# One unbroken run for a pair's step, three silu buffers, a tenth raw buffer, and gathers that begin later

## The chip, the cores and the metric

The kernel runs on one core of a Trainium2 chip, as one launch. The metric is device time in microseconds (us). Three runs of the kernel before gave 1726.6, 1728.15 and 1728.6 us, median 1728.15 us. A fourth execution was profiled: 1726.18 us, of which the profile spans 1724.4 us, at a mean granted TensorE clock of 0.989. In texts and rows PE is TensorE, DVE is VectorE, ACT is ScalarE, POOL is GpSimd and SP is SyncE; L171 is line 171 of the kernel before.

## The reference

A trunk of two layers over 256 tokens of width 1024. Only the end of the second layer is changed, a mixture of experts, top 2 of 8, each expert a SwiGLU of width 3584:

```
def _moe(h, router_w, wg, wu, wd):
    t = h.reshape(b * s, d)
    logits = einsum('td,de->te', t, router_w)
    vals, idx = lax.top_k(logits, TOP_K)
    w = jax.nn.softmax(vals, axis=-1)
    gate = sum(one_hot(idx, N_EXPERTS) * w[..., None], axis=1)
    for e in range(N_EXPERTS):
        y = y + gate[:, e:e+1] * (silu(t @ wg[e]) * (t @ wu[e])) @ wd[e]
...
        x = x + _moe(h, router_w[j], exp_w_gate[j], exp_w_up[j], exp_w_down[j])
    return _rms_norm(x, norm_final_g)
```

Before it stand a mixer with four branches in each layer and a dense SwiGLU in the first layer; they end at about 842 us of the span and are the same in both kernels.

## The kernel before

**Tiling.** The device counts the tokens of each expert and sorts the experts by load (`in_places`). The four largest, `q[0]` to `q[3]`, are taken singly, with up to 128 token places each. The four smallest are taken as two pairs, `p[0]` and `p[1]`, 64 places an expert. An expert's work is seven steps `c` (512 of the 3584 columns). A step needs its gate weights, its up weights and its down weights, each in two pieces of 1 MB (128 x 2048 f32): six pieces for a single expert, twelve for a pair. With 28 single steps and 14 pair steps that makes 336 pieces. `PAIRS` says where pair steps stand: after the single steps number 2, 4, ... 26 and 27. The last step is `p[1]`, c=6.

**Weights.** `Stream` loads pieces in the order of `pieces(steps)` from SP's queue into a ring of raw buffers: four of `rawp` and `NX`=5 of `rawx`, nine in all. A single expert's piece is split: ACT copies it to `wh` (L164), DVE subtracts to `wl` (L171), with three buffers of each, and then its raw buffer is free; PE makes three products of each 128 rows (`mm3`, L196, L197, L198). A pair's piece is used raw (`rawn`, loaded at L1088) by PE in fp32 (L1302), and its buffer is free after the last of its products. Two pieces are begun ahead of the products in work (`ahead=2`). The last 14 pieces are loaded in quarters, so 56 loads of 256 KB.

**Order.** PE, ACT and DVE run in the order in which the program is written (`manual_schedule`), so an instruction that waits holds up all that is written behind it on its engine. A step of the loop (L1361) is: gate products, silu (L1372), transposes of the previous step's result (`act_T`, L243 and the copies L214 or L1319), up products, multiplication, then the down products of the previous step, whichever kind that was. Between the pieces `tick()` runs one of the waiting `units`: eight parts of a gather (L1222), the comparison that makes the selection matrix `dm` (L1207), its transposes and gate values (`back`, L1244, L1253), or a scatter of a finished expert's output (L1335).

**The ends.** The first expert's tokens are gathered in one go (`gather_now`: 32 products, 8 copies by ACT) once both halves of the tokens are routed. In step 0 stand `in_places()`, `gates()` and the first `back`. Three groups are gathered later: `p[0]` with `q[1]` from step (q0,0), `p[1]` with `q[2]` from (q1,3), and `q[3]` from (q2,3). At the end come the last down products (`p[1]`, c=6), a Sqrt on ACT (L1393, ahead of them), the last scatters, the final norm and four output transfers on SP (L1418).

Of the kernel before, what the change touches and what calls it, by code (L numbers as in the profile page):

```python
# [34 lines left out]
NX = 5  # L35
# [29 lines left out]
def trunk(ctx: ExitStack, tc: tile.TileContext, x, pos, invf, rows, cols, wst, w_a, w_kvf, w_gate, w_br,  # L65
# [863 lines left out]
    class Routed:  # L929
# [48 lines left out]
        def meanwhile(self, pmm, psp, step):  # L978
# [4 lines left out]
            elif step == 1:  # L983
                self.products(1, 0, 4)
                self.finish(0, 1)
                self.tokens(0)
                self.gained(0, 1)
            elif step == 2:
                self.products(0, 4, 8)
                self.choose(0)  # L990
            else:
                self.wps = [psp.tile([P, 512], F32, tag="sm", name="wps") for _ in range(NT)]
                for t in range(NT):
                    nc.tensor.matmul(self.wps[t][:, :NE], ones if t else excl, self.sel[:, 0], start=True, stop=not t)
                self.place(0)
                self.tokens_hi(0)
                self.tokens_lo(0)

        def end(self, psp):
# [6 lines left out]
            nc.tensor.matmul(self.wps[1][:, :NE], excl, self.sel[:, 1], start=False, stop=True)  # L1006
            self.begin(self.third, hi=True)
            self.place(1)
# [19 lines left out]
        def place(self, t):  # L1028

            nc.vector.scalar_tensor_tensor(self.where[:, t], self.wps[t][:, :NE], 1.0, self.sel[:, t], op0=OP.add,  # L1030
                                           op1=OP.mult)

            if t == 0:
                self.dm = const.tile([P, NT, 2, P], F32R, tag="dm", name="dm")
# [15 lines left out]
    def experts(l, mine):  # L1050
# [3 lines left out]
        with ExitStack() as c2:  # L1054
# [3 lines left out]
            gf = lw.tile([P, D], F32, name="gf")  # L1058
            nc.sync.dma_start(gf, bass.AP(tensor=gfin.tensor, offset=gfin.offset, ap=[[0, P], [1, D]]))
# [5 lines left out]
            class Stream:  # L1065
# [3 lines left out]
                def __init__(self, srcs, ahead=2, whole=False):  # L1069
                    self.srcs, self.begun, self.ready, self.ahead = list(srcs), [], [], ahead  # L1070
                    self.whole = whole

                def begin(self):
                    (w, q, *rest), parts = self.srcs.pop(0)
# [7 lines left out]
                    if q < NB or self.whole:  # L1082
                        self.begun.append(load_hi(src, parts=parts, pool=pool))
                    else:
                        raw = pool.tile([P, 4 * W], F32, tag="raw", name="rawn")
                        n = 4 * W // parts
                        for i in range(parts):
                            nc.sync.dma_start(raw[:, i * n:i * n + n], src[:, i * n:i * n + n])  # L1088
                        self.begun.append(raw.rearrange("p (k n) -> p k n", k=4))

                def fill(self):
                    while (self.srcs or self.begun) and len(self.ready) <= self.ahead:
                        if not self.begun:
                            self.begin()
                        b = self.begun.pop(0)
                        self.ready.append(load_lo(*b) if isinstance(b, tuple) else b)

                def get(self):
                    self.fill()
                    return self.ready.pop(0)  # L1100
# [58 lines left out]
            class Expert:  # L1159
# [3 lines left out]
                def __init__(self, *at, base=0):  # L1163
                    self.at, self.pair, self.base = at, len(at) > 1, base
                    self.y = [None, None]
# [12 lines left out]
            def run(steps, groups, stream, tagx):  # L1178


                with ExitStack() as c3:
# [13 lines left out]
                    def slots_of(group):  # L1195


                        dm = const.tile([P, NT, 2, P], F32R, tag="dm", name="dm")
                        for i, x in enumerate(group):
                            n = P // len(x.at)  # L1200
                            for j, q in enumerate(x.at):
                                wc = whereq[:, :, q:q + 1]
                                if x.base:
                                    ws = const.tile([P, NT, 1], F32, tag="ws", name="ws")
# [313 lines left out]
```

## Time and profile before

| | |
|---|---|
| median of three runs | 1728.15 us |
| profiled execution, its own time | 1726.18 us |
| its span | 1724.4 us |
| PE busy | 1675.1 us (97%) |
| DVE busy | 1054.3 us (61%) |
| ACT busy | 830.5 us (48%) |
| bytes moved by DMA | 497.69 MB, mean 289 GB/s |

The busy shares are means over stages of different kinds. The profile page cuts the span into 40 equal slices of 43.1 us and gives for each the busy share of every engine and the GB/s that the DMA engines moved; the experts take the slices from the 20th on. The chain of waits is read backwards from the last instruction: at each step it names what the instruction waited for. A timeline lists an engine's instructions with their start, their time and, in brackets, the idle time before them and what ended it. An fp32 product of PE is recorded twice, so 16 products stand as x32.

### The profile page before, as it was taken

To read this page: it belongs to the slowest core of one execution; us is meant where nothing else is said; L and a number is where in the kernel's file an instruction comes from. 1 tells how busy PE (TensorE), PEld (TensorE's weight loads), DVE (VectorE), ACT (ScalarE), POOL (GpSimd) and SP (SyncE) were. 2 spreads that over 40 slices of the span, in tenths; PEclk is the share of its full clock that TensorE was granted. 3 is DMA by queue.
4 is the path that set the end of the run, shared out by engine and by line. 5 is a ranking of instruction groups with operands and counts; after the bars stand their busy time and mean duration, and the time that the engine had idled before them with its cause. 6 is when DMAs were issued, how large, how long until landed. Compare 5 with 4: busy or idle time off the path is not lost.

```text
span 1724.4 us, 20366 instructions
## 1 busy us (share of the span) xinstructions
PE 1675.1 (97%) x7800; PEld 1215.4 (70%) x7800; DVE 1054.3 (61%) x1282; ACT 830.5 (48%) x884; POOL 12.1 (1%) x28
## 2 busy tenths in 40 slices
PE   8999999999999999999999999999999999999996
PEld 6888888888887888888776565656656565655652
DVE  6779976555545678986675455536456544735534
ACT  6656454544434566445474444435444443534433
POOL 1000000000000000000000000000000000000000
PEclk9999999999999999999899999999999999999998
DMA  7444445555553643454668999999999999999996
GB/s 274 171 147 146 172 149 193 196 185 181 176 190 123 244 147 123 171 183 175 277 244 322 421 421 422 421 421 418 416 421 421 421 421 421 421 421 421 421 397 231
DMA packets 77818, 497.69 MB, mean 289 GB/s; under 512 B 8752, under 2 KB 8800, under 8 KB 20368
## 3 DMA queue, kind: packets, MB, share of 16 engines
q1 hardware_dynamic: 76752, 493.45, 72.8%
q0 software_dynamic: 960, 2.85, 0.6%
q8 instruction: 63, 1.03, 0.2%
q14 instruction: 43, 0.35, 0.1%
HBM read 495.22 MB, written 1.05 MB: 288 GB/s over the span
## 4 chain that ended last, share of the span: by engine, by line
PE 47%; DMA 9%; DVE 4%; ACT 3%; issue 1%; ACTq 0%; SPq 0%; DVEq 0%
DMA raw<-in_e_d 5%; PE yps L1302 4%; PE gps L1302 4%; PE ups L1302 3%; PE zps L196 3%; PE zps L198 3%; PE zps L197 3%; PE gps L196 3%; PE gps L197 3%; PE yps L197 3%; DVE wl L171 3%; PE gps L198 2%; PE yps L196 2%; PE yps L198 2%; ACT wh L164 2%; PE ups L196 2%
## 5 line engine op out<-in xcount | busy, mean ns | idle before, releaser
L171 DVE TENSOR_TENSOR wl<-raw,wh 128x2048 fp32r<-128x2048 f32 (+1 forms) x312 | 681.9, 2195 | 342.4 <-ACT wh L164 342.2
L164 ACT ACTIVATE wh<-raw 128x2048 fp32r<-128x2048 f32 (+1 forms) x312 | 571.1, 1838 | 406.1 <-PE zps L198 76.4
L196 PE MATMUL zps<-wh,hh 128*128 128x512 f32 (+1 forms) x544 | 215.7, 397 | 2.9 <-ACT wh L214 1.7
L197 PE MATMUL zps<-wl,hh 128*128 128x512 f32 (+1 forms) x544 | 209.5, 385 | 0.9 <-DVE wl L215 0.9
L198 PE MATMUL zps<-wh,hl 128*128 128x512 f32 (+1 forms) x544 | 209.6, 385 | 0.0
L215 DVE TENSOR_TENSOR al<-ps_t,ah 128x512 fp32r<-128x512 f32 x42 | 28.4, 688 | 181.0 <-ACT ah L214 180.8
L196 PEld LDWEIGHTS zps<-wh,hh 128*128 128x128 f32 x544 | 102.7, 189 | 23.7 <-ACT wh L214 2.1
L1372 ACT ACTIVATE act<-gps 128x512 f32<-128x512 f32 x42 | 25.1, 598 | 195.0 <-PE gps L1302 171.7
L197 PEld LDWEIGHTS zps<-wl,hh 128*128 128x128 f32 x544 | 102.7, 189 | 21.4 <-DVE wl L215 2.5
L198 PEld LDWEIGHTS zps<-wh,hl 128*128 128x128 f32 x544 | 102.5, 188 | 20.7
L1302 PE MATMUL ups<-rawn,xs 128*64 128x512 f32 x448 | 101.6, 597 | 1.6 <-DMA rawn<-in_e_u 1.6
L503 DVE SCALAR_TENSOR_TENSOR cacc<-ypad,col,cacc 128x256 f32<-128x256 f32 x240 | 101.4, 478 | 0.0
L1302 PE MATMUL yps<-rawn,aT 128*64 128x512 f32 x448 | 100.3, 596 | 0.0
L1302 PE MATMUL gps<-rawn,xs 128*64 128x512 f32 x448 | 100.3, 596 | 0.0
L197 PE MATMUL yps<-wl,ah 128*128 128x512 f32 x224 | 91.4, 408 | 6.7 <-DVE wl L171 6.5
L196 PE MATMUL yps<-wh,ah 128*128 128x512 f32 x224 | 92.0, 411 | 2.0 <-ACT wh L164 2.0
L196 PE MATMUL ups<-wh,xb 128*128 128x512 f32 x224 | 91.6, 409 | 0.0
L197 PE MATMUL gps<-wl,xb 128*128 128x512 f32 x224 | 88.8, 397 | 2.2 <-DVE wl L171 2.0
L198 PE MATMUL yps<-wh,al 128*128 128x512 f32 x224 | 90.4, 404 | 0.0
L196 PE MATMUL gps<-wh,xb 128*128 128x512 f32 x224 | 90.1, 402 | 0.0
L198 PE MATMUL ups<-wh,xb 128*128 128x512 f32 x224 | 88.6, 395 | 0.0
L198 PE MATMUL gps<-wh,xb 128*128 128x512 f32 x224 | 88.4, 394 | 0.0
(311 smaller groups left out, 2408.6 us busy)
## 6 DMA issues: line engine op xcount, KB each, us to landing
raw<-in_e_g SPq DMA_DIRECT2D x56, 1024.0 KB, 13.6
raw<-in_e_u SPq DMA_DIRECT2D x56, 1024.0 KB, 13.6
raw<-in_e_d SPq DMA_DIRECT2D x54, 1024.0 KB, 11.9
rawn<-in_e_g SPq DMA_DIRECT2D x52, 1024.0 KB, 12.7
rawn<-in_e_u SPq DMA_DIRECT2D x52, 1024.0 KB, 16.2
rawn<-in_e_d SPq DMA_DIRECT2D x52, 1024.0 KB, 14.1
raw<-in_w_gate SPq DMA_DIRECT2D x32, 1024.0 KB, 4.7
raw<-in_w_a SPq DMA_DIRECT2D x28, 1024.0 KB, 4.8
```

Source lines behind the costliest of these rows:

```text
L164: nc.scalar.activation(hi[:, sl], raw[:, sl], AF.Copy)
L171: nc.vector.tensor_sub(lo[:, sl], raw[:, sl], hi[:, sl].bitcast(F32))
L196: nc.tensor.matmul(ps, xh, wh, start=first, stop=False)
L197: nc.tensor.matmul(ps, xh, wl, start=False, stop=False)
L198: nc.tensor.matmul(ps, xl, wh, start=False, stop=last)
L215: nc.vector.tensor_sub(lo, src, hi.bitcast(F32))
L503: nc.vector.scalar_tensor_tensor(cacc[:, b], src, wcol, cacc[:, b], op0=OP.mult, op1=OP.add)
L1302: nc.tensor.matmul(ps[js], lhs(k)[:, js], w[:, kk], start=k == 0, stop=k == ktot - 1)
L1372: nc.scalar.activation(a, gps, AF.Silu)
```

## The change

A pair's step becomes one run: its own previous down products, then its gate, then its up products, twelve pieces with nothing between them. The single steps keep their form (gate, transposes, up, down of the previous single step); the transposes of the pair's result are made in the single step behind it. Silu's results get three buffers, the ring a tenth raw buffer (`NX`=6). The first gather's units are queued at the end of step 0 and not in it; `gates()` moves to step 1 and the first `back` behind that gather; `p[1]` is gathered alone from (q2,1) and `q[2]` alone from (q1,3). `gather_now` makes the products of the first token half ahead of the second half's places, in four PSUM banks, and ACT and DVE share the copies. A loop sees to it that an expert's gather is complete before its first product. Quarters are used for the last 6 pieces. At the end the Sqrt stands ahead of the last single step's transposes and down products. The gain vector of the final norm is loaded at the end, and two of the four output transfers go out by ACT's queue. Names at new lines: L1318 are the raw fp32 products, L1211 the comparison (tile `dms`), L1335 the copy of a pair's transposes, L1381 silu, L1435 the Sqrt.

```
-NX = 5
+NX = 6
...
             def pieces(steps):
-                order, last = [], None
-                down = lambda x, c: [(e_d, q, c, dc) for dc in range(2) for q in x.at]
+                order, last = [], [[], []]
                 for x, c in steps:
-                    order += [(w, q, c, h) for w in (e_g, e_u) for h in range(2) for q in x.at]
-                    if last:
-                        order += down(*last)
-                    last = x, c
-                return order + down(*last)
+                    into = [(w, q, c, h) for w in (e_g, e_u) for h in range(2) for q in x.at]
+                    order += last[1] + into if x.pair else into + last[0]
+                    last[x.pair] = [(e_d, q, c, dc) for dc in range(2) for q in x.at]
+                return order + last[0] + last[1]
...
-                    def gather_now(group, dm):
...
+                    def gather_now(x, dm):
+                        token_tiles([x])
+                        x.got = KD
+                        banks = [(4 * g, part, py.tile([P, 4, P], F32, tag="y", name="gaps0"))
+                                 for g in range(2) for part in range(2)]
+                        for t in range(NT):
+                            if t:
+                                mine.slot(psm, t)
+                            for k0, part, ps in banks:
+                                for i in range(4):
+                                    k = k0 + i
+                                    nc.tensor.matmul(ps[:, i], mine.parts[t][part][:, k * P:(k + 1) * P], dm[:, t, 0],
+                                                     start=not t and not i, stop=t == NT - 1 and i == 3)
...
+                    def gate_up(x, meanwhile=None):
+                        gps = pgu.tile([P, 512], F32, tag="gu", name="gps")
+                        into(x, gps)
+                        a = wk.tile([P, 512], F32, tag="act", name="act", bufs=3)
+                        nc.scalar.activation(a, gps, AF.Silu)
+                        if meanwhile:
+                            meanwhile()
+                        ups = pgu.tile([P, 512], F32, tag="gu", name="ups")
+                        into(x, ups)
+                        nc.vector.tensor_mul(a, a, ups)
+                        return a
...
                     for n, (x, c) in enumerate(steps):
...
+                        while x.got < KD:
+                            tick()
+                        if x.pair:
+                            down_of(1)
+                            prev[1] = x, c, gate_up(x)
+                            continue
+                        def meanwhile():
+                            if not x.base:
+                                if n == 0:
+                                    in_places()
+                                if n == 1:
+                                    gates()
+                                if n in groups and n:
+                                    gather(groups[n])
+                            for pair in (1, 0):
+                                turned(pair)
+                        a = gate_up(x, meanwhile)
+                        down_of(0)
+                        prev[0] = x, c, a
                         if n == 0 and not x.base:
-                            in_places()
-                            gates()
-                            units.append(lambda: back([x], mine.dm))
...
+                            gather(groups[n])
+                            units.append(lambda x=x: back([x], mine.dm))
                     nc.scalar.activation(frs[:, 0:1], epsc, AF.Sqrt)
+                    if prev[1]:
+                        stream.ahead = 1
+                        turned(0)
+                        down_of(0, between=lambda: turned(1))
...
-                            nc.sync.dma_start(out[t * P:(t + 1) * P, dc * W:(dc + 1) * W], o[t][dc])
+                            (nc.sync if dc else nc.scalar).dma_start(
+                                out[t * P:(t + 1) * P, dc * W:(dc + 1) * W], o[t][dc])
...
-                      ((q[0], 0, [p[0], q[1]]), (q[1], 3, [p[1], q[2]]), (q[2], 3, [q[3]]))}
+                      ((q[0], 0, [p[0], q[1]]), (q[2], 1, [p[1]]), (q[1], 3, [q[2]]), (q[2], 3, [q[3]]))}
-            order[-14:] = [(s, 4) for s, _ in order[-14:]]
+            order[-6:] = [(s, 4) for s, _ in order[-6:]]
```

What the change does to an engine's order stands in three places. The first is DVE about the first expert's step 0 and 1, in the kernel before: `whereq` are the token places, `lg` to `over_i` the gate values, `gs` the first expert's gates, `dm` the selection matrix of the next gather.

```order
L1117 TENSOR_REDUCE whereq<-tmp 128x16
L1139 TENSOR_SCALAR lg<-lg,rs 128x8 x2
...
L1157 CAST over_i<-over 128x9
L171 TENSOR_TENSOR wl<-raw,wh 128x2048
L1257 TENSOR_REDUCE gs<-gsps 128x1
L1207 TENSOR_TENSOR dm<-slots,whereq 128x2x64 x2
L1207 TENSOR_TENSOR dm<-slots,whereq 128x2x128
```

The same place on DVE in the changed kernel:

```order
L1122 TENSOR_REDUCE whereq<-tmp 128x16
L171 TENSOR_TENSOR wl<-raw,wh 128x2048 x2
L1386 TENSOR_TENSOR act<-act,ups 128x512
L171 TENSOR_TENSOR wl<-raw,wh 128x2048
L1211 TENSOR_TENSOR dms<-slots,whereq 128x2x64 x2
L1211 TENSOR_TENSOR dms<-slots,whereq 128x2x128
L171 TENSOR_TENSOR wl<-raw,wh 128x2048
L1144 TENSOR_SCALAR lg<-lg,rs 128x8 x2
```

The selection matrix now stands behind three subtractions `wl`, and the gate values behind a fourth.

The second place is PE at a pair's step in the middle of the program, in the kernel before: `gps`, `ups` and `yps` are the PSUM tiles of gate, up and down, `ps_t` that of the transposes.

```order
L1302 MATMUL gps<-rawn,xs 64x512 x16
L243 MATMUL ps_t<-ident,act 128x128 x4
L1302 MATMUL ups<-rawn,xs 64x512 x16
L196 MATMUL yps<-wh,ah 128x512
...
L198 MATMUL ups<-wh,xb 128x512
L1302 MATMUL yps<-rawn,aT 64x512 x16
L196 MATMUL gps<-wh,xb 128x512
```

And in the changed kernel:

```order
L198 MATMUL yps<-wh,al 128x512
L1318 MATMUL yps<-rawn,aT 64x512 x16
L1318 MATMUL gps<-rawn,xs 64x512 x16
L1318 MATMUL ups<-rawn,xs 64x512 x16
L196 MATMUL gps<-wh,xb 128x512
L197 MATMUL gps<-wl,xb 128x512
```

The three groups of raw products, which had other work between them, stand in one row, and the single expert's products in one row behind them.

The third place is ACT at the end of the program, in the kernel before: `ah` and `aT` are the copies of a single expert's and a pair's transposes, `yh` the scaled output, `frs` the Sqrt.

```order
L1372 ACTIVATE act<-gps 128x512
L214 ACTIVATE ah<-ps_t 128x512
L164 ACTIVATE wh<-raw 128x512 x8
L217 ACTIVATE yh<-yps,gs 128x512
L1319 ACTIVATE aT<-ps_t 128x512
L217 ACTIVATE yh<-yps,gs 128x512
L1393 ACT_TABLE_LOAD
L1393 ACTIVATE frs<-epsc 128x1
```

And in the changed kernel:

```order
L1381 ACTIVATE act<-gps 128x512
L164 ACTIVATE wh<-raw 128x512 x8
L1435 ACT_TABLE_LOAD
L1435 ACTIVATE frs<-epsc 128x1
L214 ACTIVATE ah<-ps_t 128x512
L217 ACTIVATE yh<-yps,gs 128x512
L1335 ACTIVATE aT<-ps_t 128x512
L217 ACTIVATE yh<-yps,gs 128x512 x3
```

The copy `ah`, which the last single step's down products need, stood ahead of the eight quarter copies and stands now behind them, the table load and the Sqrt.

## Rows read from the trace of the kernel before

**Rows 1.** Page, GB/s of the DMA engines in 40 slices of the span.

```profile
GB/s 274 171 147 146 172 149 193 196 185 181 176 190 123 244 147 123 171 183 175 277 244 322 421 421 422 421 421 418 416 421 421 421 421 421 421 421 421 421 397 231
```

**Rows 2.** Chain of waits, 970 to 1030 us: start us, us, what.

```profile
974.97 7.02 PE gps L1302 x32
981.99 0.59 PE ps_t L243 x4
982.58 7.02 PE ups L1302 x32
...
1022.72 1.93 ACT wh L164
1024.67 2.30 DVE wl L171
```

**Rows 3.** Timeline of PE, 1030 us: start us, us, instruction, [idle before <-releaser].

```profile
1030.96 7.09 PE L1302 MATMUL gps<-rawn,xs 128*64 128x512 f32 x32
```

**Rows 4.** Windows: stretch; us, busy of PE, PEld, DVE, ACT, POOL; PEclk, DMA share, GB/s.

```profile
975.00:1000.00 25.00, 25.00 (x113) 13.31 (x114) 12.66 (x7) 12.55 (x8) 0.00 (x0) 1.00 1.01 421
850.00:862.00 12.00, 12.00 (x47) 10.61 (x48) 6.06 (x5) 4.67 (x10) 0.00 (x0) 0.57 0.45 176
868.00:872.00 4.00, 0.23 (x3) 0.00 (x0) 3.31 (x18) 2.15 (x3) 0.00 (x0) 1.00 0.55 229
872.00:876.00 4.00, 3.99 (x12) 3.24 (x13) 3.86 (x12) 1.93 (x2) 0.00 (x0) 0.57 0.01 2
```

**Rows 5.** Page part 6, DMA issues: count, KB each, median us to landing.

```profile
raw<-in_w_gate SPq DMA_DIRECT2D x32, 1024.0 KB, 4.7
```

**Rows 6.** Timeline of PE, 850 to 873 us, the first expert.

```profile
850.00 0.39 PE L1006 MATMUL wps<-sel,excl 128*128 128x8 f32 x2 [1.65 <-DVE sel L1016]
...
853.16 3.71 PE L1222 MATMUL gaps<-dm,hl 128*128 128x128 f32 x16
856.66 0.73 PE L196 MATMUL gps<-wh,xb 128*128 128x512 f32 x1
...
867.85 0.38 PE L1244 MATMUL dps<-ident,dm 128*128 128x128 f32 x2
872.01 0.53 PE L1253 MATMUL gsps<-gts,dm 128*128 128x2 f32 x2 [3.78 <-DVE gts L1149]
```

**Rows 7.** Chain of waits, 914 to 922 us, the first pair's first products.

```profile
916.66 3.58 PE gps L1302 x16
```

**Rows 8.** SP's issues of the tile `raw`, 928.3 to 929.1 us.

```profile
L163 SPq DMA_DIRECT2D raw<-in_e_u x1: 328/328/328, 928.6 to 928.6; - x1
...
DMA to landing us min/median/max: 8.4/8.4/8.4
```

**Rows 9.** Timeline of PE, 1145 us, the second gather's first part.

```profile
1145.09 1.13 PE L1222 MATMUL gaps<-dm,hh 128*128 128x256 f32 x4 [2.93 <-DVE dm L1207]
```

**Rows 10.** Chain of waits, 1640 to 1722 us, two of the last loads.

```profile
1652.28 16.16 DMA rawn<-in_e_g
...
1684.84 5.67 DMA raw<-in_e_d
```

**Rows 11.** Timeline of ACT, 1690 to 1701 us.

```profile
1690.59 5.30 ACT L164 ACTIVATE wh<-raw 128x512 fp32r<-128x512 f32 x8 [8.91 <-DMA raw<-in_e_d]
...
1698.82 1.28 ACT L1393 ACT_TABLE_LOAD   x1
1700.12 0.20 ACT L1393 ACTIVATE frs<-epsc 128x1 f32<-128x1 f32 x1
```

**Rows 12.** Timeline of PE, 1691 to 1710 us, the last down products.

```profile
1691.27 0.49 PE L196 MATMUL yps<-wh,ah 128*128 128x512 f32 x1 [0.33 <-ACT wh L164]
...
1701.50 6.23 PE L1302 MATMUL yps<-rawn,aT 128*64 128x512 f32 x28
...
1708.80 1.08 PE L1302 MATMUL yps<-rawn,aT 128*64 128x512 f32 x4
```

**Rows 13.** Timeline of SP, 1700 to 1725 us, the outputs.

```profile
1716.13 2.58 SPq L1418 DMA_DIRECT2D out_x<-o  x4
```

More of the change, by code (lines that the diff above doesn't have):

```diff
@@ L991, in meanwhile @@
             else:
[L992 to L995, printed above, removed]
+                self.slot(psp, 0)
                 self.tokens_hi(0)
@@ L1081, in begin @@
                     turn[0] += 1
-                    if q < NB or self.whole:
-                        self.begun.append(load_hi(src, parts=parts, pool=pool))
+                    if self.split[i]:
+                        self.ready[i] = load_lo(*load_hi(src, parts=parts, pool=pool))
                     else:
@@ L1086, in begin @@
                         n = 4 * W // parts
[L1087 to L1096, printed above, removed]
-                def get(self):
-                    self.fill()
-                    return self.ready.pop(0)
+                        for j in range(parts):
+                            nc.sync.dma_start(raw[:, j * n:j * n + n], src[:, j * n:j * n + n])
+                        self.ready[i] = raw.rearrange("p (k n) -> p k n", k=4)
+                def get(self):
+                    i = self.n
+                    self.n += 1
+                    while self.next < len(self.order) and self.next <= self.at[i] + self.ahead:
+                        full = sum(self.split[j] for j in self.ready) == 3
+                        if full and self.split[self.order[self.next]] and i in self.ready:
+                            break
+                        self.begin()
+                    return self.ready.pop(i)
             gate, mx, e8 = small("gate", NT, NE), small("mx", 2, NT), small("e8", NT, NE)
@@ L1310, in into @@
                             products(x, ps, lhs, 4 * h, KD)
-                            if h == 0:
+                            if h == 0 and not x.pair:
                                 tick(1 + (len(units) > 6))
@@ L1339, in down @@
                     def down(x, c, lhs, between=None, last=None):
-                        if c == NFC - 1:
+                        if c == NFC - 1 and not between:
                             while any(hasattr(u, "scatter") for u in units) or late:
@@ L1347, in down @@
                                 x.y[dc] = py.tile([P, 512], F32, tag="y", name="yps")
-                            if dc:
+                            if dc and (between or not x.pair):
                                 (between or tick)()
@@ L1373, in run @@
+                        down_of(0)
+                        prev[0] = x, c, a
                         if n == 0 and not x.base:
-                            in_places()
-                            gates()
-                            units.append(lambda: back([x], mine.dm))
-                        if n in groups:
                             gather(groups[n])
-                        if prev is not None:
-                            alhs = act_T(prev[0], prev[2])
-                        if end and not x.base:
-                            stream.ahead = 1
@@ L1383, in run @@
-                        ups = pgu.tile([P, 512], F32, tag="gu", name="ups")
-                        into(x, ups)
-                        nc.vector.tensor_mul(a, a, ups)
-                        ahead = []
-                        if prev is not None:
-                            down(*prev[:2], alhs, (lambda: ahead.append(act_T(x, a))) if end else None)
-                        prev = (x, c, a)
-                    while units or late:
-                        tick()
-                    nc.scalar.activation(frs[:, 0:1], epsc, AF.Sqrt)
+                            units.append(lambda x=x: back([x], mine.dm))
@@ L1397, in add, with rest @@
                             scatter(x, dc, t)()
-                    down(x, c, *ahead, last=lambda: add(0))
+                    def rest():
+                        while units or late:
+                            tick()
+                        add(0)
+                    down_of(x.pair, between=lambda: tick(2), last=rest)
                     add(1)
```

86 lines of the change are left out of this document (49 added, 37 removed).

## The prediction

> **What bounds the kernel now.** I read first the page's slices. From the 23rd to the 38th the DMA engines move 416 to 422 GB/s [rows 1], and a window inside has a DMA share of 1.01 [rows 4]: from about 925 us almost to the end the weights arrive as fast as this trace ever shows. A piece of 1,048,576 bytes at 421 GB/s takes 2.49 us, the 24 pieces between two pair steps 59.8 us.
>
> Next, the chain of waits over one such cycle, for what PE needs in the same time. A pair's gate products begin at 974.97 and the next pair's at 1030.96 [rows 2, 3], 56.0 us apart. Three raw stretches take 7.02 us each, transposes 0.59, so two single steps take 56.0 - 21.06 - 0.59 = 34.4 us. PE has some 3.7 us to spare in each cycle. In the same cycle PE is busy all of a 25 us window [rows 4], yet the queue decides, since PE works off pieces that came earlier. The 97% of the page hides this.
>
> So the end is the moment from which the ring stays fed, plus the pieces left at 2.49 us, plus a tail behind the last weights. Work that PE saves in the middle is worth nothing; what keeps the queue busy sooner, and what is done behind the last landing, counts in full.
>
> Then the three places. Start: from 850 to 862 us the DMA share is 0.45, from 872 to 876 it is 0.01 [rows 4]. Here DMA waits for buffers and PE sets the pace. The 30th piece, the second up piece behind the first pair's gate and up, is issued at 928.6 and lands 8.4 us later, at 937.0 [rows 8]; from it on the landings are evenly spaced. Tail: the first quarter of the last single expert's down weights lands at 1690.5 [rows 10], the last raw product ends at 1709.9 [rows 12]. Last the outputs, four issues by SP from 1716.13, the last ending at 1718.7 [rows 13].
>
> **Start: -8.0 us (-10 to -5).** Before, all 32 products of the first gather stand behind the wait of 1.65 us for `sel`; the first weight product follows at 856.66 [rows 6]. After, 16 of them fit ahead of that wait. Sixteen take 3.7 us [rows 6], so the second sixteen, begun at about 850.2, end near 853.9: -2.8. From 850 to 862 the clock is 0.57 [rows 4], behind that wait; with work before it PE may keep full clock, and the 12 us hold about 5 us of loss, of which I count half: -2.4 (none to 5).
>
> In step 0 PE waits 3.78 us for the gate values `gts` [rows 6] and then runs at 0.57 for 4 us [rows 4], which at full clock would need some 2.3: 3.8 + 1.7, with the small products beside it 0.4 more, -5.9, since `gates()` moves a step on, behind a fourth `wl`. What is late next is `dms`, now behind three subtractions of 2.30 us [rows 2]; behind it on DVE stand the fourth `wl` and the gate values, and PE's next split products wait for that `wl`. The nearest row is the later gather's wait of 2.93 us for `dm` [rows 9]; the bounds are nothing (subtractions done before PE arrives) and 3 x 2.30 = 6.9. I take 3.5, near the row, 1.0 for half clock behind it and 1.2 for small waits. The last gather part and the transposes `dps` now come ahead of the first pair: +0.9 (1.13 at half clock [rows 9], 0.38 [rows 6]). So the pair begins -2.8 - 2.4 - 5.9 + 3.5 + 1.0 + 1.2 + 0.9 = -4.5, at 912.2 in place of 916.66 [rows 7].
>
> With nine buffers the 30th piece took over the buffer of the 21st, an up piece that comes free after 7.0 (gate), transposes and half an up stretch: issue at 928.6. With ten it takes that of the 20th, a gate piece, free when the gate stretch ends: 912.2 + 7.0 = 919.2, landing 8.4 us later [rows 8] at 927.6 in place of 937.0: -9.4. The first run of split products carries the gather's last units and a wait; by the reckoning of a cycle below that is E of some 8.8, 1.4 over the bound: -8.0. Upper bound -5: `dms` at its 6.9; lower -10: no hole and the clock at full.
>
> **Middle: +2 us (-1 to +5).** Between pair runs PE now does twelve split pieces in a row. Follow the ring through a cycle. The run's first piece is landed, then copied (1.92) and subtracted (2.30) [rows 2]: +4.2. The single steps take 34.4, the transposes 0.6. Half a raw stretch, 3.5 us, frees the first pair buffers; a load without a queue ahead takes 4.7 us to land [rows 5]. That is 47.4 us plus E, the cycle's other work on PE. With ten buffers that load is the piece 22 behind the run's first (12 split pieces and ten), due, at 2.49 us each, after 54.8 us. So the queue is kept busy as long as E stays below 7.4 us. Ordinary cycles have a few small products. A gather has eight parts of some 0.6 us, transposes, and a wait for its matrix of 2.9 us [rows 9]: 8 to 9 us, over the bound by 1 to 2. There are three later gathers in place of two. PE's idle time ahead of a run can also come with a half clock, as behind the wait in step 0. I take +2: one overrun and the restart behind it. Lower bound: slices of 418 and 416 in place of 421 [rows 1] cost (3 + 5)/421 x 43.1 = 0.8 us, which may go. Upper bound: all three gathers over by 1.7.
>
> The Trainium skill, "Perfetto Trace Analysis", section Optimization Strategy, says that where the most-contended engine changes over time, interleaving the regimes may help. That speaks against this change, which sets raw work (short of data) and split work (short of PE) apart. The rule gives no price; its case is the slower rival below.
>
> **Whole pieces: -2.2 us (-2.5 to 0).** Before, 32 quarters of the last gate and up weights land between 1668.4 (1652.28 + 16.16) and 1690.5 [rows 10]: 22.07 us for what takes 8 x 2.49 = 19.9 in whole pieces. These become whole. The price is that PE waits for whole pieces, but the pair's up products then end within the time that the two following split pieces land. Zero if the lost time belongs to the end of the queue and not to the quarters.
>
> **Tail: +6.3 us (+4 to +8).** Reckon from the landing of the last quarter of the split pieces. Eight quarter copies end at 1690.59 + 5.30 = 1695.9 [rows 11], each 0.66, so that landing is at 1695.2. Before, the down products start on the first quarter (1691.27) and the raw ones end at 1709.9 [rows 12], 14.65 us behind it. After, `ah` stands behind all eight copies, the table load and the Sqrt: 0.66 + 1.28 + 0.20 [rows 11] + 0.67 for `ah`, as for the like-sized scaled copy, + some 0.15 of handing over = 2.95 us. Then 24 products at 0.235 (5.6), transposes 0.6, raw products 7.3 (6.23 + 1.08 [rows 12]), scatters in two PSUM banks 2.5, and 1.6 more since PE sat idle for about 4 us and restarts at half clock, as at 872 [rows 4]; 0.4 between groups. 20.95 against 14.65. Bounds: +4.5 without the half clock, +8 if it lasts twice as long.
>
> The trace has the next ACT instruction 1.30 us behind the start of the table load [rows 11]. The Trainium skill, "ScalarE: Activation LUTs", section What ACT_TABLE_LOAD costs, gives about 2.66 us for a switch, load and drain. By the page the tail would be 1.4 us longer and the sum -2.2; by the row the load is its own 1.28 us and nothing more, and the sum goes by the row.
>
> **Outputs: -1.7 us (-2 to 0).** Four issues take 2.58 us on SP [rows 13]; with two on ACT the last is issued two steps of 0.65 earlier, 1.3, and some 0.4 for overlapping ends. Zero if the last transfer waits for DVE's last result anyway. Loading the gain vector late costs nothing: it lands behind the last weights, while PE has over 15 us of work. Three silu buffers cost and give nothing by themselves.
>
> **Sum.** -8.0 + 2 - 2.2 + 6.3 - 1.7 = -3.6 us. Against the profiled execution, 1726.2 of its own time with 1.8 outside the span, 1726.2 - 3.6 = 1722.6. The median lies 1.9 us above it, so 1724.5 us.
>
> **Rivals.**
> 1. The middle and the tail cost less: `ah` and the raw products overlap, the ring never runs dry. Start -9, middle 0, whole pieces -2.2, tail +4.5, outputs -1.7: -8.4, 1720 us. For it: E below 7.4 in most cycles. Against it: ACT's written order.
> 2. The gain at the start is given back. If gathers run the ring dry (+5) with a start of -6.5 and a tail of +5.5, outputs -1.7, whole pieces -2.2: 0, 1728 us. For it: PE's waits for `dm` in each gather.
> 3. Slower: the unbroken split run outlasts the ring. If waits and half clock ahead of each run make E 8.9 us in ordinary cycles, the queue stands 1.5 us in each of 12 cycles: +18, with the other terms (-5.6) +12.4, 1740 us. It decides from E = 7.4. For it: PE's spare 3.7 us a cycle must now fall at the one place where it waits for landing, copy and subtraction, and the clock fell behind such waits. Against it: half clock for some 4 us (1.7) and the small products leave E below 4.
>
> **How the numbers follow.** Less than 0.2%, 3.5 us, can't be told from no change. Forecast 0.43 (1718 to 1730 by itself; a good half of it beyond -3.5), rival 1 0.25, rival 2 0.14, rival 3 0.18. Faster 0.25 + 0.25 = 0.50, the same 0.18 + 0.14 = 0.32, slower 0.18. The range leaves out the upper half of rival 3 and the far end of rival 1: 1714 to 1736.
>
> **What would show it.** Start: first gate product near 854, no wait of 3.8 us at the gate values, a new wait of some 3.5 us for `dms`, the 30th piece landed near 928. Middle: slices of 421 GB/s but for one or two at the gathers; dips in every cycle would be rival 3. Tail: ACT's `ah` behind eight quarter copies and the table load, PE idle some 4 us ahead of the last split products, 21 us from the last split quarter to the last raw product. Outputs: two issues on each queue. The forecast is wrong if the tail is as short as before, or if the queue is not full from about 917 us.

## Result and the profile after

The changed kernel is slower: median 1748.65 us of four runs (1745.12 to 1750.92) against 1728.08 us, a ratio of 1.0121 (95% interval 1.0109 to 1.0134), +20.6 us. The prediction said 1724.5 us, with a range of 1714 to 1736 and a chance of 0.18 for slower. A later measurement of the same kernel gave 1746.4 us, 1.0117 (1.0099 to 1.0135).

The profiled execution has a span of 1749.1 us, 24.7 more than that of before. The page's slices, 43.7 us each, show where; they answer to [rows 1]:

```profile
GB/s 269 170 145 145 168 169 168 197 188 192 179 185 147 212 144 121 169 180 241 237 265 375 412 420 421 421 407 421 420 421 300 422 355 421 420 421 420 421 419 173
```

The queue is full from the 24th slice on, as before from the 23rd, and in three places it is not: 407 in the 27th slice (1.5 us of a slice), 300 in the 31st (from 1312 us), 355 in the 33rd (from 1399 us). The missing 121 and 66 of 421 GB/s are 12.6 and 6.9 us of a slice. The others up to the 38th move 420 to 422. So it is not the unbroken order in every cycle; it is mainly two stretches.

A window over a stretch of single-step products between two raw runs shows them. I call such a stretch a run; the four below are an ordinary one, the two bad ones, and the one behind. Columns as in [rows 4]:

```profile
989.90:1024.09 34.19, 34.19 (x157) 28.11 (x157) 25.85 (x16) 19.71 (x14) 0.00 (x0) 1.00 1.01 419
1285.75:1340.98 55.23, 46.80 (x203) 37.45 (x202) 34.89 (x27) 25.98 (x22) 0.00 (x0) 0.91 0.92 378
1337.00:1350.00 13.00, 12.79 (x60) 5.99 (x60) 2.75 (x7) 1.23 (x3) 0.00 (x0) 0.87 0.22 83
1363.50:1409.38 45.88, 40.37 (x181) 32.36 (x181) 28.72 (x21) 20.61 (x17) 0.00 (x0) 0.96 0.99 405
1488.64:1524.24 35.60, 35.60 (x163) 29.23 (x162) 30.05 (x20) 22.80 (x17) 0.00 (x0) 1.00 1.01 420
```

An ordinary run takes 34 to 40 us; one takes 44.5 and lost under 2 us (the 407). That of 55.2 us holds the four scatters of the second expert and the whole gather of the second pair. At its end and in the raw products behind it (third row) PE is busy, but the DMA share is 0.22. The one of 45.9 us holds the scatters of the first pair and half of the fourth expert's gather. What PE waited for in the run of 55.2 us (what waits, for what, us in total, times, longest):

```profile
PE gaps L1226 <- DVE dms L1211: 2.6, 1, 2.6
PE sps L1351 <- DVE x_sb L1353: 2.2, 1, 2.2
PE gps L197 <- DVE wl L171: 1.8, 1, 1.8
PE gps L196 <- ACT wh L164: 0.8, 1, 0.8
PE ps_t L243 <- ACT aT L1335: 0.7, 1, 0.7
```

The mean granted clock of the run is 0.91: of its 55.2 us some 10 pass at the half level, in three stretches, which costs 5 us. On SP's timeline one group of loads lies across the stall: four issues take 17 us. The ring is then full of a pair's pieces, whose buffers come free only with the raw products behind the run.

```profile
1330.34 16.93 SPq L1093 DMA_DIRECT2D rawn<-in_e_u  x4
```

The start answers to [rows 6, 8]. The first weight product is at 857.48, no earlier than the 856.66 of before; PE waits for `dms` (2.9 us), then for a copy of gathered tokens; the 30th piece is issued at 925.8 and lands 8.3 us later, at 934.1 in place of 937.0:

```profile
852.39 0.54 PE L1027 MATMUL wps<-sel,ones 128*128 128x8 f32 x2
...
857.48 0.73 PE L196 MATMUL gps<-wh,xb 128*128 128x512 f32 x1
```

```profile
PE gaps L1226 <- DVE dms L1211: 2.9, 1, 2.9
PE gaps L1226 <- ACT xb L1235: 1.8, 1, 1.8
```

The chain at the end answers to [rows 10 to 12]:

```profile
1706.85 5.33 DMA raw<-in_e_d
1712.20 0.63 ACT wh L164
1712.85 1.28 ACT L1435
1714.35 0.49 ACT ah L214
1714.88 0.79 PE yps L196
1715.68 0.43 PE yps L197
...
1733.69 1.06 PE yps L1318 x4
```

The last split quarter lands at 1712.2, the copy, the table load and `ah` follow each other on ACT as the order has them, PE starts at 1714.88 and its first twelve products stand 0.43 us apart where 0.24 is usual. The last raw product ends at 1734.7, 22.5 us behind that landing; before it was 14.65.

The 24.7 us, landing by landing, against the same pieces of the kernel before: -2.9 at the 30th piece; +2.2 more by the 185th, in gaps of 1.6 us at most; +20.2 between the 185th and the 233rd (the two stalls: 73.1 and 66.5 us for 24 pieces each, where 59.8 is the full rate); -2.5 from there to the last split quarter, of which the whole pieces are some 2; +7.9 in the tail; -0.1 behind the last raw product. Sum 24.8.

### The profile page after: what moved, and what is told of

Its sections match the earlier page's. It is cut to its first block, busy times and chain, and to the rows that moved or that the text cites. A ratio compares the mean times of both kernels' runs of the same rounds, so it can differ in the third digit from the quotient of the medians.

```text
span 1749.1 us, 20350 instructions
## 1 busy us (share of the span) xinstructions
PE 1678.4 (96%) x7832; PEld 1233.3 (71%) x7832; DVE 1054.1 (60%) x1284; ACT 828.6 (47%) x879; POOL 12.1 (1%) x28
## 4 chain that ended last, share of the span: by engine, by line
PE 51%; DMA 6%; DVE 3%; ACT 3%; issue 1%; ACTq 0%; SPq 0%; DVEq 0%
PE yps L1318 6%; DMA raw<-in_e_g 4%; PE gps L197 3%; PE yps L196 3%; PE yps L197 3%; PE yps L198 3%; PE gps L196 3%; PE gps L198 3%; PE zps L196 3%; PE zps L198 3%; PE zps L197 3%; PE gps L1318 3%; PE ups L1318 3%; PE ups L196 3%; PE ups L197 3%; PE ups L198 3%
## 5 line engine op out<-in xcount | busy, mean ns | idle before, releaser
L1381 ACT ACTIVATE act<-gps 128x512 f32<-128x512 f32 x42 | 25.1, 598 | 297.5 <-PE gps L1318 254.6
L198 PEld LDWEIGHTS zps<-wh,hl 128*128 128x128 f32 x544 | 102.5, 189 | 20.6
L197 PE MATMUL gps<-wl,xb 128*128 128x512 f32 x224 | 93.2, 416 | 11.0 <-DVE wl L171 11.0
L1318 PE MATMUL ups<-rawn,xs 128*64 128x512 f32 x448 | 101.0, 593 | 2.7 <-DMA rawn<-in_e_u 2.7
L1318 PE MATMUL yps<-rawn,aT 128*64 128x512 f32 x448 | 101.4, 604 | 0.0
L1318 PE MATMUL gps<-rawn,xs 128*64 128x512 f32 x448 | 98.6, 592 | 0.0
L196 PE MATMUL gps<-wh,xb 128*128 128x512 f32 x224 | 94.3, 421 | 3.3 <-ACT wh L164 3.3
L198 PE MATMUL gps<-wh,xb 128*128 128x512 f32 x224 | 92.6, 413 | 0.0
L197 PE MATMUL ups<-wl,xb 128*128 128x512 f32 x224 | 88.8, 397 | 0.0
```

The lines of the kernel that those rows point to most:

```text
L196: nc.tensor.matmul(ps, xh, wh, start=first, stop=False)
L197: nc.tensor.matmul(ps, xh, wl, start=False, stop=False)
L198: nc.tensor.matmul(ps, xl, wh, start=False, stop=last)
L1318: nc.tensor.matmul(ps[js], lhs(k)[:, js], w[:, kk], start=k == 0, stop=k == ktot - 1)
L1381: nc.scalar.activation(a, gps, AF.Silu)
```

## Experiments

Theory A: the end is set by two runs that outlast the ring, by ACT's order in the tail and by `dms` at the start; the rest of the change costs nothing. B: the unbroken run costs in every cycle. The other rivals are named where they are tested. The ratios are to the kernel before. The "control" is the changed kernel again, 1746.4 us; its two bad runs are 52.1 and 47.4 us long where the first trace has 55.2 and 45.9. The eight times of the changed kernel lie between 1745.1 and 1750.9, so a difference of 2 or 3 us between medians of four is within the scatter, and there the landings of the profiled execution have to decide.

**The control.**

> The changed kernel itself, as the measure for the others: 1743 to 1751 us. In its first trace two runs of single-step work, of 44.5 and 55.2 us, were 3.4 us longer than the same runs of the four kernels after it (41.1 and 52.2), in which nothing was altered there but in one of them. If that was chance it shows 41 and 52 too, and about 1745.

1746.4 us, 1.0117 (1.0099 to 1.0135). The run of 52.1 us has the same five waits as that of 55.2, but a mean granted clock of 0.97 in place of 0.91:

```profile
1284.12:1336.20 52.08, 43.63 (x203) 35.19 (x203) 34.81 (x27) 26.00 (x22) 0.00 (x0) 0.97 0.96 394
```

That accounts for the 3.1 us: 9% of 55.2 is 5.0 us lost to the clock, 3% of 52.1 is 1.7. It is so with the shorter runs too (44.5 us at 0.92, 41.3 at 1.00; 45.9 at 0.96, 47.4 at 0.93). Why the clock falls behind a wait in one execution and not in the next stays open.

**The fourth expert's gather later.**

```
-    (q[2], 3, [q[3]])
+    (q[2], 5, [q[3]])
```

> The fourth expert's gather is queued at (q2,5) and not at (q2,3); all else as in the changed kernel. Theory A (two overfull runs): the trace of the changed kernel has 13 stretches of single-step work between two raw runs; those of 34 to 40 us leave the queue full, one of 55.2 us and one of 45.9 us outlast it and cost some 19 us. The one of 45.9 falls to about 39, the one behind it grows from 37.6 to about 43, the stall of some 7 us there goes: about 1742 us (-6). Rival B (the unbroken run costs in every cycle, wherever a gather stands): no change, 1748 +- 2.

1738.47 us, 1.0066 (1.0049 to 1.0083), -8 from the control. The run is 37.0 us and the queue full through it and through the next, of 40.0 us; the second stall is gone:

```profile
1357.31:1394.34 37.03, 36.29 (x164) 29.58 (x165) 28.10 (x20) 19.81 (x14) 0.00 (x0) 1.00 1.01 421
1415.16:1455.15 39.99, 37.39 (x182) 30.71 (x181) 28.48 (x18) 23.28 (x21) 0.00 (x0) 1.00 1.01 420
```

Nothing in the order of a pair's step was altered, so B falls. (The recorded forecast of 43 us for the next run was 3 too long.)

**The second pair's matrix a run ahead.**

```
+    early = []
...
-    dm = slots_of(group)
+    dm = early.pop() if early else slots_of(group)
...
+    if (x, c) == (q[2], 0):
+        units.append(lambda: early.append(slots_of([p[1]])))
```

> Only the selection matrix of the second pair's gather is made earlier, in the step (q2,0), one run ahead; its products stay. Theory A: PE's wait of 2.6 us for it and the half clock behind it (1.7) go from the overfull run, 55.2 to 51 us, and the stall of 11.4 to about 7: about 1744.5 us (-4.3). Rival B: the wait was cover for something that is late anyway (the subtractions), no change, 1748 +- 2.

1740.69 us, 1.0073 (1.0056 to 1.0090), -5.7. The wait for `dms` is absent from the run's waits, the run is 47.9 us, and from the 185th to the 209th piece 63.8 us pass in place of the control's 68.0: the -4.3 that was expected. The rest of the median's difference lies within the scatter of the runs. Of the 4.3 the 2.6 are the edit's. The rest is the clock, 1.00 in this run, and does not hang on the edit alone: in the trace of all four edits, below, the wait is gone too, but the clock is 0.93.

**The tail.**

```
+    if n == len(steps) - 1:
+        turned(0)
     down_of(1)
```

> The transposes of the last single step, with their copies, stand ahead of the last pair's run, and so ahead of the eight quarter copies, the table load and the Sqrt on ACT. Theory A (the tail is ACT's order): PE's idle 3.8 us and the half clock behind it go, the last split products start on the first quarter; from the last split quarter to the last raw product 16 to 17 us in place of 22.5: about 1743 us (-6). Rival C (the tail is set by the raw products behind the last landing): no more than -1.5, 1747.

1740.81 us, 1.0078 (1.0061 to 1.0095), -5.6. From the last split quarter to the last raw product 16.6 us, where the control has 22.7. The table load still stands behind the quarter copies, but no PE product of the single expert waits for it:

```profile
1703.29 5.33 ACT L164 ACTIVATE wh<-raw 128x512 fp32r<-128x512 f32 x8 [5.43 <-DMA raw<-in_e_d]
1708.64 1.28 ACT L1437 ACT_TABLE_LOAD   x1
1709.93 0.20 ACT L1437 ACTIVATE frs<-epsc 128x1 f32<-128x1 f32 x1
1710.04 0.67 ACT L217 ACTIVATE yh<-yps,gs 128x512 fp32r<-128x512 f32 x1
```

So the tail was ACT's order, not the raw products (rival C).

**The first matrix in step 0.**

```
     in_places()
+    early.append(slots_of(groups[0]))
```

The list `early` is the one of the experiment with the second pair's matrix.

> The first gather's selection matrix is made in step 0, right behind the token places and ahead of the three subtractions; its products stay in step 1. Theory A: PE's wait of 2.9 us at the first gather part goes with the half clock behind it (1.7), the first pair's run begins 3 to 4.5 us earlier, and as the end is counted in pieces from there it counts in full: about 1744.5 us (-4). Rival D: the gain at the start is swallowed by the two overfull runs or by the wait for the gate values that follows (1.8 us): at most -1, 1748.

1743.84 us, 1.0104 (1.0087 to 1.0121), -2.6. The 30th piece lands at 928.9, 3.9 before the control's, and the last split quarter 3.8 before it. The wait for `dms` is gone; the copy's 1.8 us stays:

```profile
PE gaps L1226 <- ACT xb L1235: 1.8, 1, 1.8
PE gps L197 <- DVE wl L171: 1.3, 1, 1.3
```

The trace says -4, the median -2.6 with an interval that holds both; rival D (-1) is not excluded by the median alone, but by the landings, which keep the gain to the end. In the six traces with ten buffers and without this edit the 30th piece lands at 932.8 to 935.1, in the four with it at 928.9 to 930.5.

**Nine buffers.**

```
-NX = 6
+NX = 5
```

> The ring has nine raw buffers in place of ten; all else as in the changed kernel. Theory A says how long a run of single-step work the queue outlasts: 42 us with ten buffers, so 39.5 with nine. Runs of 41.1, 45.9 and 52 us lose 1.6 to 2.5 us more each, two of about 40 lose 0.7, the start 2.5: about +10, 1755 us where the changed kernel has 1745. Rival E (the tenth buffer is of no use behind the start): +2.5 only.

1753.78 us, 1.0149 (1.0131 to 1.0167), +7.4 from the control's median, +5.1 from that of the first measurement: not 10, but more than rival E's 2.5. The 30th piece lands 3.6 later; a run of 44.1 us now stalls by 2.7 and 1.5, where the first trace with ten buffers lost 1.6 at one of 44.5.

**The second pair's gather early.**

```
-NX = 6
+NX = 5
-    tag="xs", name="xs", bufs=1
+    tag="xs", name="xs", bufs=2
-    (q[2], 1, [p[1]]), (q[1], 3, [q[2]])
+    (q[1], 3, [p[1], q[2]])
```

> Nine raw buffers, two buffers for a pair's tokens (so that the second pair's may be gathered while the first pair's are in use), and the second pair gathered with the third expert from (q1,3), as before the change; all else as in the changed kernel. Theory A: against nine buffers alone the stall at the run of 52 us goes (-11), the run with the gather of both is 2 to 3 us longer than 41 and stalls by 4: about 1747. Rival B (the unbroken run, not the place of the gather): within 2 us of nine buffers alone, 1753 or more.

1746.84 us, 1.0110 (1.0092 to 1.0128), -6.9 from nine buffers alone, as A has it. The run ahead of the second pair is 37.7 us and free (53.5 with nine buffers alone, a stall of 12); in return one of 42.2 us behind the gather of both stalls by 3.3, one of 40.9 by 1.4. The gather's work is the same; what it costs hangs on which run it falls into.

**One part of the change alone, in the kernel before.** The buffer counts and the counting in `got` are left out here.

```
-    (q[1], 3, [p[1], q[2]])
+    (q[2], 1, [p[1]]), (q[1], 3, [q[2]])
...
+    while n and c == 0 and x.got < KD:
+        tick()
```

> The kernel before (interleaved order, nine raw buffers) with one part of the change alone: the second pair gathered by itself from (q2,1) and the third expert by itself from (q1,3), the gather completed ahead of the pair's first product; three buffers for dT and one for al make room. Theory A (the late gather overfills the cycle ahead of the second pair's first step, in either order): the interleaved cycle has some 4 us to spare, the gather with its wait and the scatters bring 15 to 20: slower than the kernel before by 6 to 12 us, 1734 to 1740. Rival F (only the unbroken run makes a late gather dear): within 3 us of before.

1732.96 us, 1.0026 (1.0015 to 1.0037), +4.9: between the two forecasts, with an interval (2.6 to 6.4 us) that touches both. Between the 185th and the 233rd piece this kernel loses 4.6 us (124.0 in place of 119.4); the unbroken order loses 21.0 there with nine buffers and 16.9 (control) to 20.2 with ten. But that stretch holds the fourth expert's gather too, and in the unbroken order an early gather costs something in the runs before it. As a price of the late gather by itself, late against early with nine buffers, the medians give 4.9 us in the interleaved order and 6.9 in the unbroken one (the two experiments above). A over-estimated the late gather by itself. Rival F may have a part of the truth, that the interleaved order spreads the same work over more landings, but 2 us between two such differences do not show it. One row of the stretch:

```profile
1285.00:1345.00 60.00, 58.30 (x266) 39.11 (x264) 37.23 (x33) 27.92 (x23) 0.00 (x0) 0.97 0.98 405
```

**The length of a run by itself.** Idle transposes on PE are added to two ordinary runs of the changed kernel.

```
+    for at, count in (((q[0], 5), 46), ((q[3], 0), 111)):
+        if not x.base and (x, c) == at:
+            ps = psm.tile([P, 4, P], F32, tag="sm", name="extra")
+            for i in range(count):
+                nc.tensor.transpose(ps[:, i % 4], ident, ident)
```

> The changed kernel with idle work on PE added in two ordinary runs: 46 transposes of the identity (5 us) in step (q0,5), 111 (12 us) in step (q3,0); the results are not used. So far a run of L us has cost about L - 43.8 (55.2: 11.4; 52.2: 8.2; 50.9: 6.9; 47.9: 4.1). Theory A: 34.2 + 5 = 39.2 is free, 35.6 + 12 = 47.6 costs 3.8 us: +4 from the changed kernel's 1746.4, 1750. Rival G (each us of PE work in an unbroken run costs a us): +17, 1763. Rival H (the gather's traffic or waits, not the length): +0 to +1.

1754.25 us, 1.0153 (1.0137 to 1.0168), +7.9. The run of 39.2 us is free, the one of 47.7 costs 7.0 us (24 pieces in 66.8 us in place of 59.8), with no gather in it, no wait and the clock at full:

```profile
990.52:1029.72 39.20, 39.20 (x203) 33.12 (x203) 25.85 (x16) 19.82 (x14) 0.00 (x0) 1.00 1.01 421
1485.70:1533.42 47.72, 47.72 (x274) 41.35 (x273) 30.21 (x20) 22.90 (x17) 0.00 (x0) 1.00 1.00 398
1533.42:1545.00 11.58, 11.58 (x55) 3.93 (x56) 0.00 (x0) 0.00 (x0) 0.00 (x0) 1.00 0.65 255
```

That settles that length alone does it (against H) and that there is a threshold (against G, +17). The size was a miss: 3.8 by the fit L - 43.8, 5.7 to 5.9 by the prediction's reckoning (a bound of 42), 7.0 measured; the landings say why, as the next part tells under the middle.

**All four edits.** The edits of the first four experiments together, with ten buffers.

> The four single edits together, with ten buffers: fourth expert's gather at (q2,5), the second pair's matrix a run ahead, the last single step's transposes ahead of the last pair's run, the first matrix in step 0. Theory A: the effects stand in different places and add up, -6.5 - 4.3 - 6 - 4 = -21 from the changed kernel, 1724 us where that has 1745; the run of 52 falls to 48 and is the last that stalls, by 4 us or so. Rival D (gains swallow one another in the queue): 1732 or more.

1725.5 us (ten runs), 0.9987 (0.9977 to 0.9997): the four add up, -20.9 from the control, where the four medians by themselves give -21.9. So the four places are worth as much as the change lost. The run ahead of the second pair is the last that stalls by more than 2 us, with 7.2 by the landings:

```profile
1281.38:1332.24 50.86, 45.06 (x203) 36.37 (x202) 34.49 (x25) 25.97 (x22) 0.00 (x0) 0.93 0.97 403
```

**Further.** One unit a place while scatters wait, the fourth expert's matrix a run ahead, quarters for the last 8 pieces, all outputs on SP.

```
-    tick(1 + (len(units) > 6))
+    tick(1 + (len(units) > 6 and not hasattr(units[0], "scatter")))
+    if (x, c) == (q[2], 3):
+        units.append(lambda: early.append(slots_of([q[3]])))
-    order[-6:] = [(s, 4) for s, _ in order[-6:]]
+    order[-8:] = [(s, 4) for s, _ in order[-8:]]
-    (nc.sync if dc else nc.scalar).dma_start(
+    nc.sync.dma_start(
```

> The four edits together, and four more: one unit a place while scatters wait (the doubled ones made PE wait 2.2 us for a PSUM bank), the fourth expert's matrix a run ahead, quarters for the last 8 pieces in place of 6, all outputs on SP. Theory A: the run of 50.9 us falls to 47 (-3.5 of its stall of 6.9), that of 43 to 40 (-1.7), the last up products start on quarters (-1.5), the outputs by SP -0.5: -7 from 1725.5, about 1718 us, faster than the kernel before by 0.5%. Rival D: the queue sets the end and takes these gains back, 1724 or more.

1724.64 us (eleven runs), 0.9981 (0.9972 to 0.9990), clear of the kernel before by a little. The run ahead of the second pair is 48.3 us (expected 47), again at a clock of 0.93, and its stall 4.6 by the landings; the run of 43 is 37.1. Of the expected -7 about -1 came in the median; the profiled spans differ by -2.8. By the trace the last split quarter comes 2.9 sooner, but the tail is 16.7 us in both: with quarters PE is done with the last up products sooner, and then waits 2.5 us, where it waited 0.8, for the multiplication of the pair's result, which stands on DVE behind eight quarter subtractions:

```profile
PE ps_t L243 <- DVE act L1388: 2.5, 1, 2.5
```

**One piece ahead at the last pair.**

```
     if n == len(steps) - 1:
         turned(0)
+        stream.ahead = 1
```

> The further mended kernel with one piece begun ahead in place of two during the last pair's step, so that on DVE the multiplication of the last pair's result stands behind four quarter subtractions and not eight. Theory A: the wait of 2.5 us that PE has for it between the last single expert's two down pieces goes, the tail is 14.3 us in place of 16.7: about 1722.3 us (-2.4), 0.9967 of the kernel before. Rival I (the tail is set by the landing of the last quarters): within 0.5 of 1724.6.

1723.13 us (six runs), 0.9968 (0.9956 to 0.9980): the lowest median, below the kernel before by 0.32%; its interval and that of the version above overlap. The wait is gone; the tail is 15.6 us in place of 16.7, so some 1.1 of the 2.4 came. By the trace the raw products begin 1.9 sooner behind the last split quarter, and their second stretch of twelve takes 0.8 longer (3.57 in place of 2.8), with the last quarters landing while it runs; that it waits for them was not tested. That the median is as forecast is in part luck: the run ahead of the second pair had a clock of 1.00 in this trace, 0.93 in the other. It is the same fault as that of `ah` and `dms`: a small instruction behind copies that wait for data.

## Why the prediction was wrong

**The bound** was right: landings at 2.49 us, the end counted from them. Every microsecond of the difference was found as a gap between landings or behind the last one.

**Middle, +2 (-1 to +5): this step failed; the trace has +22.4 (2.2 and 20.2).** Of the 28.3 us between the forecast for the span (-3.6) and the trace (+24.7) 20.4 are here. The mechanism was right: a run of single-step work is free up to a length, and what goes beyond is lost. What failed is E, the cycle's other work on PE. I put one gather of "8 to 9 us" into one run and left the rest as "a few small products". The orders show what stands in the run ahead of the second pair: a whole gather with its transposes, because the guard finishes it before the pair, the wait of 2.6 us for its matrix, the four scatters of the second expert, with a wait of 2.2 us of their own, and some 5 us lost at half clock. That is 20.8 us above the 34.4. The next run has the first pair's four scatters and half of the next gather, 11.5 us above. I had the price of each piece and did not ask which of them fall into one cycle. Rival 3 had the sign and, for the middle, nearly the amount (+18), but put it in all cycles; two did it.

The bound of 42 us failed too, though less: it is not one number. By the landings a run behind quiet cycles lost what it had above some 43.9 us (52.1 us lost 8.2, 47.9 lost 4.0; that of 55.2 lost 13.3, but the raw products behind it took 1.7 longer at half clock). The run directly behind an overfull one lost all above 39 (45.9 lost 6.7, 47.4 lost 8.5), and 39 is what a cycle has for its run: 59.8 us for 24 landings less 20.8 for the raw products. An estimate from these numbers: pieces landed ahead are a store of some 5 us, an overfull run empties it, and a quiet cycle refills it by what its run has below 39. The run of 47.7 us with added transposes had only one run of 37.6 us between it and a stall, which refills 1.4: 47.7 - 39.0 - 1.4 = 7.3, where 7.0 was measured. So the second run's stall is in part the first one's doing. The fit L - 43.8 had left the second runs out. No run was made to test the store by itself.

The Trainium skill, "Perfetto Trace Analysis", section Optimization Strategy, says that interleaving regimes may help. The runs agree for this place in part: between the 185th and the 233rd piece the interleaved order with the late gather lost 4.6 us and the unbroken one 16.9 to 21.0, though the late gather by itself is worth 4.9 and 6.9. They do not for ordinary cycles, which run at the full rate in either order.

**Start, -8.0: -2.9.** Here the first gather failed. I gave it -2.8 for its place and -2.4 for the clock; the first weight product came 0.8 later than before, at 857.48, and the clock from 850 to 862 us is 0.59 where it was 0.57 (0.72 in the control). The first half of the products is done at half clock in front of the second half's places (`wps` at 852.39 where it was 850.00), and the second half then waits for its own selection matrix. From trace to trace that first product lies between 855.8 and 857.5, so it is no gain in any of them beyond 0.9. The rest, from it to the pair, came as reckoned: 60.8 us, where the prediction without the clock has 60.7. In it the wait for `gts` went, `dms` came in its place with 2.9 us (3.5 taken), and a wait of 1.8 us for a copy of gathered tokens, where I had 1.2 for everything small. The pair's run begins at 918.25 and not at 912.2; before it was 916.66 [rows 7]. The -2.9 is mostly the tenth buffer's (with nine the piece lands at 936.4, before at 937.0). With `dms` moved the 30th piece is at 928.9, 8.1 before 937.0. That it equals the -8.0 is luck: it comes from a wait that the prediction had as a cost.

**Whole pieces, -2.2:** -2.1 by the landings. The last pair's eight gate and up pieces take 19.9 us where the 32 quarters took 22.0 (21.6 in the second trace of the order before, the one with the late gather). It was not tested alone.

**Tail, +6.3 (+4 to +8): +7.9.** Mechanism right, shown by taking it away (-6.1 in the trace). Too small by the half clock behind PE's wait of 3.8 us for `ah`: twelve products took 5.4 us in place of 2.8, 2.6 lost where I took 1.6. The table load cost 1.28 us on the path and the next ACT instruction came 1.29 us after its start, as before.

**Outputs, -1.7: -0.1.** ACT's first issue took 1.70 us and held up its own second scaling behind it. (The row names DVE for the idle 1.77 us, but DVE's `o` was done at 1741.83; the issue ended at 1742.66.)

```profile
1740.96 1.70 ACTq L1472 DMA_DIRECT2D out_x<-o  x1
1742.70 0.72 ACT L1468 ACTIVATE o<-o,frs 128x512 f32<-128x512 f32 x1 [1.77 <-DVE o L1469]
```

**Chances.** Four terms of the sum erred in the same direction: middle by 20.4 us, start by 5.1, tail and outputs by 1.6 each. The range was built as if errors were small and independent.

Open: why the clock falls behind a wait in one execution and not in another. Also open is what the unbroken order by itself is worth: no run has the interleaved order with ten buffers, and none has the unbroken order as the only change.

## What to carry to other kernels

Where a ring of buffers feeds two kinds of work in turn, work out how long the consumer may hold it, in landings, and list for every single run, from the order of the changed program, what stands in it; the sum of the fullest run decides, not the mean. Two full runs in a row cost more than two apart, since the first uses up what had landed ahead (6.7 us here for a run of 45.9 us behind one of 55.2). A unit that "must be done before X" gathers all late work in front of X. An instruction put behind copies that wait for data (a matrix for a gather, a copy at the end) waits for that data too: place it before them.

## What was not expected of the hardware

The first DMA issue from ACT's queue took 1.70 us (1.69 to 1.72 in the control and two more traces), the second 0.34; SP's output issues took 0.35 to 1.3. With outputs on both queues the last issue ended 9.1 us behind the last raw product, with all on SP 8.8 to 9.3.

The same program with the same waits was granted a mean clock of 0.91 in a run of one trace and 0.97 in the same run of another, which is 3 of its 55 us.
